# Conditions of a decoder trunk: 128x1024 blocks on GpSimd, layer 3's beside the retention, wider value products

## The chip, the cores and the metric

One core of one Trainium2 chip runs the whole kernel. The metric is device time in microseconds, the median of the runs shown. A profiled execution of the same program gives the trace.

## What is computed

A trunk of four layers over 512 tokens of width 1024, batch 1, in fp32. Layer i mixes tokens by latent attention (MLA, layers 0 and 3), stick-breaking attention (layer 1) or retention (layer 2); behind each mixer stands a dense MLP with squared ReLU and 4096 hidden units (FFN). Every mixer and FFN is wrapped in RMS norms and in a condition of the sequence: shift, scale and gate, six vectors of 1024 a layer.

```python
cond = jax.nn.silu(c)                          # (1, 1024)
for i in range(DEPTH):                         # 4
    mod = cond @ ada_w[i] + ada_b[i]           # 1024 x 6144
    sh_a, sc_a, g_a, sh_f, sc_f, g_f = jnp.split(mod, 6, axis=-1)
    h = modulate(rms_norm(x, norm_g[i, 0]), sh_a, sc_a)
    y = ...mixer(h)...
    x = x + g_a[:, None, :] * rms_norm(y, norm_g[i, 1])
    h = modulate(rms_norm(x, norm_g[i, 2]), sh_f, sc_f)
    y = jnp.square(jax.nn.relu(h @ ffn_w1[i])) @ ffn_w2[i]
    x = x + g_f[:, None, :] * rms_norm(y, norm_g[i, 3])
```

## The kernel before

**Products.** Each fp32 operand is split into a high and a low part, and each product is three TensorE matmuls into one PSUM bank (mm3, L90 to L92). A weight block of 128x1024 (512 KB) is loaded by `load_w` (L100) into a buffer `raw`, cast by ScalarE to its high part `wh` (L84), and VectorE subtracts to get the low part `wl` (L85). There are four buffers `raw`, seven each of `wh` and `wl`. Each block feeds 24 matmuls of 512 columns.

**Order.** The program is written as Python generators, and a scheduler in the build puts the instructions of each engine in an order, which the engine keeps. All DMAs of loads stand on one queue, SP's, in that order: a load that waits for its buffer holds back every load behind it. The scheduler also decides which of the four buffers a load takes.

**Conditions.** The generator `ada` runs beside a mixer or an FFN and is moved on one step (`next(bg)`) after each weight load. A group is one vector's half, 512 columns: four loads of 512 KB into `raw` (L258, two row blocks of 128x512 each), and on VectorE a multiply (L272) and seven multiply-adds (L274) into `adaacc`. `column` then transposes (L306) and reduces (L308) on VectorE, folds with a small matmul (L311) and adds the bias (L315). A gate is turned into a row by TensorE (L324), written to DRAM (L328) and read back over all partitions (L332). 44 groups run in this way; the shift and scale of the first mixer are made at the start, by the same generator in another mode. In FFN l the conditions of layer l+1 are computed. An instruction that is `held` is kept, in the scheduler's order, behind a certain matmul early in the FFN.

**Norms.** At the end of each mixer and FFN the output blocks of 128 tokens (tb 0 to 3) pass through a norm of y and then a norm of the new x: ScalarE sums the squares (ssy, ssx, L135), GpSimd makes var and rstd (L127, L130), and VectorE scales. TensorE then transposes the normed x (xn, L365) for the next product, two blocks of tokens at a time.

**Values.** In the attention heads, `to_T` transposes the probabilities by TensorE, splits them, and `av` multiplies with the values (L876), in two halves of the queries.

Of the kernel before, what the change touches and what calls it, by code (L numbers as in the profile page):

```python
# [14 lines left out]
P = 128  # L15
# [27 lines left out]
class Trunk:  # L43
    def __init__(self, ctx, tc, ins, out, mixers):
# [13 lines left out]
        self.adap = pool("ada", 2)  # L58
# [175 lines left out]
    def ada(self, wanted):  # L234

        nc = self.nc
        groups = list(wanted)  # L240
        if not groups:
            return
        raws, due = {}, []

        def load(n):
            if n >= 4 * len(groups):
                return
            l, part, name, half = groups[n // 4]
            col = (3 * part + self.ROWS[name]) * D + half * 512
            w = self.d_ada_w[l].rearrange("(kb p) n -> p kb n", p=P)  # L250
            c = n % 4
            if self.starting:
                raws[n] = [self.u(name="adaw") for _ in range(2)]
                for i in (0, 1):
                    nc.sync.dma_start(out=raws[n][i], in_=w[:, 2 * c + i, col:col + 512])
                return
            raw = self.raw().rearrange("p (a b) -> p a b", a=2)
            nc.sync.dma_start(out=raw, in_=w[:, 2 * c:2 * c + 2, col:col + 512])  # L258
            raws[n] = [raw[:, i] for i in (0, 1)]

        load(0)
        for n in range(4 * len(groups)):
            load(n + 1)
            rv, c = raws.pop(n), n % 4
            l, part, name, half = groups[n // 4]
            if c == 0:
                a = self.adap.tile([P, 512], F32, tag="acc", name="adaacc")
# [8 lines left out]
            if due and (not self.starting or c == ST2):  # L276
                next(due[0], None)
            if c == 3:
                due[:] = [self.column(*groups[n // 4], a)]
            yield  # L280
        for _ in due[0]:
            pass
        yield

    def column(self, l, part, name, half, a):


        nc = self.nc
        if name == "G":
            dst = self.st(4, "gate")  # L290
            if half == 0:
                self.gates[l, part] = self.dp.tile([1, D], F32, tag=f"gate{l}{part}", name=f"gate{l}{part}")
        else:
            if half == 0:
                self.mods[l, part, name] = self.modp.tile([P, KB], F32, name=f"mod{l}{part}{name}")
            dst = self.mods[l, part, name][:, half * 4:half * 4 + 4]
        b = (6 * l + 3 * part + self.ROWS[name]) * KB + half * 4
        if self.starting:
            ps = self.trp()[:, 0:4]
            for j in range(4):  # L300
                nc.tensor.matmul(ps[:, j:j + 1], a[:, j * P:j * P + P], self.onesf[:, 0:1], start=True, stop=True)
            nc.vector.tensor_add(dst, ps, self.bcols[:, b:b + 4])
        else:

            aT = self.adap.tile([P, 512], F32, tag="aT", name="aT", bufs=1)
            self.held(nc.vector.transpose(aT, a))  # L306
            r = self.adap.tile([P, 16], F32, tag="ar", name="ar", bufs=1)
            self.held(nc.vector.reduce_sum(r, aT.rearrange("p (c i) -> p c i", i=32), axis=mybir.AxisListType.X))  # L308
            yield
            ps = self.trp()[:, 0:16]  # L310
            nc.tensor.matmul(ps, self.fold, r, start=True, stop=True)  # L311
# [1024 lines left out]
```

## Time and profile before

| | |
|---|---|
| median of 3 runs | 2563.69 us (2559.38 to 2564.23) |
| profiled execution | 2561.43 us, span 2559.6, mean granted clock 0.987 |
| TensorE matmul (PE) | 2443.5 us, 95%, 12003 instructions |
| VectorE (DVE) | 1601.5 us, 63% |
| ScalarE (ACT) | 1089.0 us, 43% |
| GpSimd (POOL) | 151.8 us, 6%, 319 instructions |
| read from HBM | 319.51 MB |

A busy time is the sum of an engine's instructions. The share is an average over parts of the program with different limits; what a part is limited by is read from what its engines wait for. A granted clock of 1.00 is 2.4 GHz, 0.50 is 1.2 GHz. A row of a window reads: start:end, length, then busy us and (instructions) of PE, PEld (TensorE's weight loads), DVE, ACT and POOL, then granted clock, share of the DMA engines, GB/s. A row of a timeline: start, us, engine, line, operation, out<-in, and in brackets the idle time before it with what ended it.

### The profile page before, as it was taken

To read this page: it belongs to the slowest core of one execution; us is meant where nothing else is said; L and a number is where in the kernel's file an instruction comes from. 1 tells how busy PE (TensorE), PEld (TensorE's weight loads), DVE (VectorE), ACT (ScalarE), POOL (GpSimd) and SP (SyncE) were. 2 spreads that over 40 slices of the span, in tenths; PEclk is the share of its full clock that TensorE was granted. 3 is DMA by queue.
4 is the path that set the end of the run, shared out by engine and by line. 5 is a ranking of instruction groups with operands and counts; after the bars stand their busy time and mean duration, and the time that the engine had idled before them with its cause. 6 is when DMAs were issued, how large, how long until landed. Compare 5 with 4: busy or idle time off the path is not lost. (4 is left out here: it accounts for less than half of the span.)

```text
span 2559.6 us, 31769 instructions
## 1 busy us (share of the span) xinstructions
PE 2443.5 (95%) x12003; PEld 2052.5 (80%) x12003; DVE 1601.5 (63%) x2664; ACT 1089.0 (43%) x2014; POOL 151.8 (6%) x319
## 2 busy tenths in 40 slices
PE   5989999999999999999999999999999999999998
PEld 4778787888887877878788887888778778888887
DVE  7996767656988677754644444487664576634434
ACT  6655332235665533223533334443223566633322
POOL 5101000001000100000100000100000220100000
PEclk9999999999999999999999999999999999999999
DMA  7353755534112375552322222376552312333331
GB/s 242 112 182 122 256 184 187 188 123 125 59 34 72 120 250 173 188 156 91 131 74 95 95 79 82 99 238 189 174 178 85 102 34 79 128 97 101 95 95 42
DMA packets 227066, 330.00 MB, mean 129 GB/s; under 512 B 15969, under 2 KB 115169, under 8 KB 226913
## 3 DMA queue, kind: packets, MB, share of 16 engines
q1 hardware_dynamic: 226912, 327.97, 40.4%
q8 instruction: 94, 1.54, 0.3%
q14 instruction: 60, 0.48, 0.1%
HBM read 319.51 MB, written 8.42 MB: 128 GB/s over the span
## 5 line engine op out<-in xcount | busy, mean ns | idle before, releaser
L84 ACT CAST wh<-raw 128x1024 fp32r<-128x1024 f32 (+1 forms) x356 | 372.5, 1052 | 632.1 <-PE acc L92 385.3
L85 DVE TENSOR_TENSOR wl<-raw,wh 128x1024 fp32r<-128x1024 f32 (+1 forms) x356 | 434.0, 1221 | 281.6 <-ACT wh L84 278.2
L91 PE MATMUL mmp<-hl,wh 128*128 128x512 f32 (+1 forms) x1408 | 520.8, 371 | 2.4 <-DVE hl L85 2.4
L90 PE MATMUL mmp<-hh,wh 128*128 128x512 f32 (+1 forms) x1408 | 519.7, 372 | 2.1 <-ACT snT L597 1.6
L92 PE MATMUL mmp<-hh,wl 128*128 128x512 f32 (+1 forms) x1408 | 519.6, 370 | 0.0
L90 PE MATMUL acc<-wh,h1h 128*128 128x512 f32 x1024 | 407.1, 398 | 22.1 <-DVE y L533 15.1
L92 PE MATMUL acc<-wh,h1l 128*128 128x512 f32 x1024 | 403.3, 394 | 0.0
L91 PE MATMUL acc<-wl,h1h 128*128 128x512 f32 x1024 | 402.8, 393 | 0.0
L274 DVE SCALAR_TENSOR_TENSOR adaacc<-raw,cond,adaacc 128x512 f32<-128x512 f32 x308 | 230.5, 748 | 120.1 <-DMA raw<-in_ada_w_dram 115.8
L91 PEld LDWEIGHTS mmp<-hl,wh 128*128 128x128 f32 x1408 | 265.4, 188 | 47.6 <-DVE hl L85 3.9
L90 PEld LDWEIGHTS mmp<-hh,wh 128*128 128x128 f32 x1408 | 263.6, 188 | 47.6 <-ACT snT L597 2.0
L92 PEld LDWEIGHTS mmp<-hh,wl 128*128 128x128 f32 x1408 | 265.3, 188 | 45.2
L90 PEld LDWEIGHTS acc<-wh,h1h 128*128 128x128 f32 x1024 | 195.3, 191 | 66.0 <-DVE y L533 17.4
L92 PEld LDWEIGHTS acc<-wh,h1l 128*128 128x128 f32 x1024 | 194.7, 190 | 41.4
L91 PEld LDWEIGHTS acc<-wl,h1h 128*128 128x128 f32 x1024 | 195.3, 191 | 39.3
L84 ACT CAST h1h<-relu 128x512 fp32r<-128x512 f32 (+1 forms) x144 | 82.5, 575 | 240.1 <-DVE relu L483 240.1
L90 PE MATMUL acc<-wh,oh 128*128 128x512 f32 x320 | 128.0, 402 | 5.6 <-ACT wh L84 3.1
L85 DVE TENSOR_TENSOR h1l<-relu,h1h 128x512 fp32r<-128x512 f32 (+1 forms) x144 | 90.5, 631 | 62.9 <-ACT h1h L84 62.6
L92 PE MATMUL acc<-wh,hl 128*128 128x512 f32 (+1 forms) x320 | 123.3, 389 | 5.2 <-DVE hl L85 4.3
L91 PE MATMUL acc<-wl,oh 128*128 128x512 f32 x320 | 127.1, 397 | 0.0
L127 POOL TENSOR_SCALAR var<-ssy 128x1 f32<-128x1 f32 x32 | 18.9, 590 | 1819.0 <-ACT junk L135 1819.0
L92 PE MATMUL acc<-wh,ol 128*128 128x512 f32 x320 | 126.2, 395 | 0.0
(291 smaller groups left out, 3596.6 us busy)
## 6 DMA issues: line engine op xcount, KB each, us to landing
raw<-in_ffn_w_dram SPq DMA_DIRECT2D x256, 512.0 KB
raw<-in_ada_w_dram SPq DMA_DIRECT2D x176, 512.0 KB
raw<-in_ret_w_in_dram SPq DMA_DIRECT2D x48, 512.0 KB
raw<-in_sb_w_in_dram SPq DMA_DIRECT2D x24, 512.0 KB
x<-x SPq DMA_DIRECT2D x48, 256.0 KB
adaw<-in_ada_w_dram SPq DMA_DIRECT2D x32, 256.0 KB
raw<-in_mla_w_out_dram SPq DMA_DIRECT2D x16, 512.0 KB
raw<-in_ret_w_out_dram SPq DMA_DIRECT2D x16, 512.0 KB
```

Of the source, the lines that this page charges most:

```text
L84: ins = self.nc.scalar.copy(hi, src)
L85: (engine or self.nc.vector).tensor_sub(lo, src, hi.bitcast(F32))
L90: first = self.mm = mm(ps, l[0], r[0], start=start, stop=False)
L91: mm(ps, l[0], r[1], start=False, stop=False)
L92: mm(ps, l[1], r[0], start=False, stop=stop)
L127: self.nc.gpsimd.tensor_scalar(v, ss, ss2, EPS, ALU.add, ALU.add)
L274: ins = nc.vector.scalar_tensor_tensor(a, rv[i], wcol, a, ALU.mult, ALU.add)
```

## The change

A job is now a layer's part with one to three vectors, and a block is 128 rows of one vector's whole 1024 columns: 22 vectors x 8 blocks = 176 loads of 512 KB, as many and as large as before. GpSimd multiplies a block in place by its rows' conditions and adds it to `adaacc` (1024 wide); neither is `held`. Transposes and reduces stay on VectorE, 44 each. One fold matmul serves a whole job (9 in place of 44), a gate is turned in one piece (8 in place of 16). The conditions of layer 3 (48 blocks) are computed beside the retention mixer of layer 2, 12 blocks a head, in place of its FFN. The scaling of the softmax's max goes from GpSimd to VectorE. `to_T` transposes key block by key block, and `av` is 12 matmuls of 512, 384, 256 and 128 columns (three each) in place of 18 of 256 and 128.

```diff
-        self.adap = pool("ada", 2)
+        self.adap = pool("ada", 1)
...
-            for i in range(2):
-                kb = 2 * c + i
-                wcol = self.cond[:, kb:kb + 1]
-                if kb == 0:
-                    ins = nc.vector.tensor_scalar(a, rv[i], wcol, None, ALU.mult)
-                else:
-                    ins = nc.vector.scalar_tensor_tensor(a, rv[i], wcol, a, ALU.mult, ALU.add)
-                self.held(ins)
...
+    def ada(self, jobs):
+        nc = self.nc
+        blocks = [(job, i, kb) for job in jobs for i in range(len(job[2])) for kb in range(KB)]
+        raws, due, sums = {}, [], {}
+
+        def load(n):
+            if n < len(blocks):
+                (l, part, names), i, kb = blocks[n]
+                col = (3 * part + self.ROWS[names[i]]) * D
+                raws[n] = self.raw()
+                nc.sync.dma_start(out=raws[n], in_=self.d_ada_w[l][kb * P:kb * P + P, col:col + D])
+
+        load(0)
+        for n, (job, i, kb) in enumerate(blocks):
+            load(n + 1)
+            if due and next(due[0], self) is self:
+                due.pop(0)
+            rv = raws.pop(n)
+            wcol = self.cond[:, kb:kb + 1]
+            if kb == 0:
+                a = self.adap.tile([P, D], F32, tag="acc", name="adaacc", bufs=2)
+                nc.gpsimd.tensor_scalar(a, rv, wcol, None, ALU.mult)
+            else:
+                nc.gpsimd.tensor_scalar(rv, rv, wcol, None, ALU.mult)
+                nc.gpsimd.tensor_add(a, a, rv)
+            if kb == KB - 1:
+                due.append(self.columns_of(job, i, a, sums))
+            yield
...
-        nc.gpsimd.tensor_scalar(m, m, -MLA_SCALE, None, ALU.mult)
+        nc.vector.tensor_scalar(m, m, -MLA_SCALE, None, ALU.mult)
...
+        for kbs in ((0,), (1, 3), (2,)):
+            ps = self.trp()
+            off, spans = 0, []
+            for kb in kbs:
+                start = off
+                for qb in range(kb, TB):
+                    nc.tensor.transpose(ps[:, off:off + P], rows[qb][:, kb * P:kb * P + P], self.ident)
+                    off += P
+                spans.append((kb, start, off))
+            hi, lo = self.u(F32R, "pTh"), self.u(F32R, "pTl")
+            self.split(hi[:, 0:off], lo[:, 0:off], ps[:, 0:off])
...
+        for kb, r in enumerate(pT):
+            self.mm3(ps[:, kb * P:512], V[kb], r, kb == 0, kb == TB - 1)
...
+            background()
             k = rotated(hd, D)
+            background()
...
             og = mix(sc, V, sg)
-            for _ in range(6):
-                next(bg, None)
...
+        beside = {0: [(0, 0, ("G",)), (0, 1, ("sh", "S"))]}
+        for l in range(1, len(mixers)):
+            if mixers[l - 1] == "ret":
+                beside[l - 1] = beside.get(l - 1, []) + [(l, p, ("sh", "S", "G")) for p in (0, 1)]
```

The scheduler's order moves with it, at two places that matter here. The first is SP's queue in the FFN of layer 0, in the third of its four quarters: loads of conditions (in_ada_w) and of weights (in_ffn_w2, in_ffn_w1), with the engines whose work each waits for. Before, condition loads wait for a buffer that VectorE frees:

```order
L258 DMA raw_3927<-in_ada_w_dram 128x2x512 [waits DMAHW3_49,DVE_49]
L100 DMA raw_3961<-in_ffn_w2_dram 128x2x512 [waits DMAHW0_49,DVE_49]
L258 DMA raw_3967<-in_ada_w_dram 128x2x512 [waits DMAHW5_49,DVE_49]
L100 DMA raw_3995<-in_ffn_w2_dram 128x2x512 [waits DMAHW2_49,DVE_49]
L258 DMA raw_4001<-in_ada_w_dram 128x2x512 [waits DMAHW7_49,DVE_49]
L100 DMA raw_4033<-in_ffn_w1_dram 128x4x256 [waits DMAHW4_49,DVE_49]
```

After, in the second quarter of the same FFN:

```order
L300 DMA raw_3337<-in_ada_w_dram 128x1024 [waits DMAHW3_49,Pool_49]
L100 DMA raw_3347<-in_ffn_w1_dram 128x4x256 [waits DMAHW6_49,DVE_49]
L300 DMA raw_3353<-in_ada_w_dram 128x1024 [waits DMAHW5_49,Pool_49]
L100 DMA raw_3421<-in_ffn_w1_dram 128x4x256 [waits DMAHW0_49,DVE_49]
L300 DMA raw_3427<-in_ada_w_dram 128x1024 [waits DMAHW7_49,DMAHW5_49,Pool_49]
L100 DMA raw_3432<-in_ffn_w1_dram 128x4x256 [waits DMAHW2_49,DVE_49]
```

What moved: a condition's load waits for GpSimd (Pool) to be done with the block before it, in the same buffer. Before, 34 steps in a row in the FFN of layer 0 have this form, condition after condition in one buffer; after, 27 steps in three runs (10, 10 and 7), and 19 in the FFN of layer 1; in the other steps conditions and weights change buffers.

The second place is GpSimd's queue at the end of layer 1's FFN, where the norms of the last two token blocks (ssy of y, ssx of x) lead to the retention. Before:

```order
L127 TENSOR_SCALAR var_11439<-ssx_11434 128x1
L130 TENSOR_TENSOR rstd_11440<-var_11439,mhalf_125 128x1
L127 TENSOR_SCALAR var_11463<-ssy_11035 128x1
L130 TENSOR_TENSOR rstd_11464<-var_11463,mhalf_125 128x1
L127 TENSOR_SCALAR var_11474<-ssx_11469 128x1
L130 TENSOR_TENSOR rstd_11475<-var_11474,mhalf_125 128x1
```

After:

```order
L313 TENSOR_SCALAR raw_11345<-raw_11345,cond_103 128x1024
L314 TENSOR_TENSOR adaacc_11339<-adaacc_11339,raw_11345 128x1024
L127 TENSOR_SCALAR var_11032<-ssx_11027 128x1
L130 TENSOR_TENSOR rstd_11033<-var_11032,mhalf_125 128x1
L127 TENSOR_SCALAR var_11056<-ssy_10628 128x1
L130 TENSOR_TENSOR rstd_11057<-var_11056,mhalf_125 128x1
L313 TENSOR_SCALAR raw_11429<-raw_11429,cond_103 128x1024
L314 TENSOR_TENSOR adaacc_11339<-adaacc_11339,raw_11429 128x1024
L313 TENSOR_SCALAR raw_11433<-raw_11433,cond_103 128x1024
L127 TENSOR_SCALAR var_11067<-ssx_11062 128x1
L130 TENSOR_TENSOR rstd_11068<-var_11067,mhalf_125 128x1
L314 TENSOR_TENSOR adaacc_11339<-adaacc_11339,raw_11433 128x1024
```

What moved: blocks of layer 3's conditions stand ahead of and between the var and rstd of the norms. At the ends of the first MLA and of the stick-breaking mixer it is the same with the first blocks for the FFN behind them.

## Rows read from the trace of the kernel before

**Rows 1.** The page: costliest groups (busy us, mean ns | idle before) and DMA issues.

```profile
L274 DVE SCALAR_TENSOR_TENSOR adaacc<-raw,cond,adaacc 128x512 f32<-128x512 f32 x308 | 230.5, 748 | 120.1 <-DMA raw<-in_ada_w_dram 115.8
...
raw<-in_ffn_w_dram SPq DMA_DIRECT2D x256, 512.0 KB
```

**Rows 2.** What TensorE waited for: us, times, longest.

```profile
PE acc L90 <- DVE y L533: 15.1, 5, 5.2
...
PE trp L324 <- DVE gate L321: 10.6, 3, 4.8
...
PE acc L90 <- ACT wh L84: 3.1, 1, 3.1
```

**Rows 3.** Windows: FFN 0, 1, retention heads, FFN 2, 3, first and last MLA's heads.

```profile
221.60:593.00 371.40, 362.75 (x1697) 302.04 (x1696) 254.49 (x402) 128.05 (x204) 7.68 (x14) 0.99 0.55 174
861.10:1234.50 373.40, 360.70 (x1690) 301.08 (x1689) 246.84 (x387) 130.72 (x208) 7.74 (x14) 0.99 0.51 162
1290.00:1600.00 310.00, 306.42 (x1432) 256.24 (x1432) 142.86 (x194) 111.45 (x180) 13.22 (x32) 0.99 0.27 85
1648.30:2025.90 377.60, 362.62 (x1698) 302.39 (x1697) 242.65 (x397) 131.16 (x210) 7.75 (x14) 0.99 0.50 158
2199.40:2551.10 351.70, 351.09 (x1646) 294.71 (x1645) 149.04 (x189) 121.26 (x185) 5.80 (x10) 1.00 0.29 89
76.80:158.10 81.30, 74.47 (x429) 63.55 (x430) 80.16 (x192) 56.56 (x140) 9.17 (x23) 0.98 0.42 129
2068.50:2138.20 69.70, 68.39 (x420) 60.90 (x421) 51.13 (x124) 54.22 (x134) 1.56 (x7) 1.00 0.01 3
```

**Rows 4.** TensorE's timeline in FFN 0, at the wait for y.

```profile
389.18 0.79 PE L90 MATMUL acc<-wh,h1h 128*128 128x512 f32 x1 [5.20 <-DVE y L533]
```

**Rows 5.** Window behind that wait.

```profile
388.10:394.90 6.80, 5.72 (x14) 4.47 (x15) 5.16 (x8) 0.00 (x0) 0.00 (x0) 0.50 0.66 207
```

**Rows 6.** TensorE's groups by shape: the folds.

```profile
L311 PE MATMUL trp<-ar,fold 128*128 128x16 f32 x88 | 13.1, 225 | 2.9 <-DVE relu L483 1.2 <-DVE pTl L85 1.1 <-DVE ar L308 0.6
```

**Rows 7.** TensorE's timeline, one head's value products in the last MLA.

```profile
2105.99 0.42 PE L876 MATMUL mmp<-pTh,vh 128*128 128x256 f32 x2
...
2108.17 0.40 PE L90 MATMUL mmp<-lath,wh 128*128 128x512 f32 x1
```

**Rows 8.** GpSimd's timeline at the start (start, us, operation).

```profile
7.67 0.52 POOL L1258 MEMSET mask<- 128x512 f32 x1
8.26 0.29 POOL L1258 TENSOR_SCALAR_AFFINE_SELECT mask<-mask 128x128 f32<-128x128 f32 x1
...
34.96 8.75 POOL L1258 TENSOR_TENSOR hl<-ht,hh 128x256 fp32r<-128x256 f32 x8
...
56.06 0.19 POOL L129 TENSOR_SCALAR var<-ssq 128x1 f32<-128x1 f32 x1 [1.68 <-ACT junk L135]
...
67.27 0.69 POOL L791 TENSOR_SCALAR wh<-wh 128x64 fp32r<-128x64 f32 x2
```

**Rows 9.** VectorE's timeline beside those eight adds.

```profile
33.06 6.90 DVE L1258 SCALAR_TENSOR_TENSOR adaacc<-adaw,cond,adaacc 128x512 f32<-128x512 f32 x7
```

**Rows 10.** SP's timeline, condition loads at MLA 0's end, in FFN 0 and FFN 2.

```profile
195.17 0.37 SPq L258 DMA_DIRECT2D raw<-in_ada_w_dram  x1
...
301.54 0.37 SPq L258 DMA_DIRECT2D raw<-in_ada_w_dram  x1
...
381.76 0.37 SPq L258 DMA_DIRECT2D raw<-in_ada_w_dram  x1
...
1756.73 0.37 SPq L258 DMA_DIRECT2D raw<-in_ada_w_dram  x1
```

**Rows 11.** VectorE's timeline, the multiply-adds that wait for the last of them.

```profile
1760.77 1.54 DVE L274 SCALAR_TENSOR_TENSOR adaacc<-raw,cond,adaacc 128x512 f32<-128x512 f32 x2 [0.49 <-DMA raw<-in_ada_w_dram]
```

**Rows 12.** GpSimd's timeline, FFN 1 to retention.

```profile
1243.95 0.60 POOL L127 TENSOR_SCALAR var<-ssx 128x1 f32<-128x1 f32 x1 [2.40 <-ACT junk L135]
```

**Rows 13.** TensorE's timeline there: transposes of normed x.

```profile
1248.28 1.47 PE L365 MATMUL trp<-ident,xn 128*128 128x128 f32 x12
```

More of the change, by code (lines that the diff above doesn't have):

```diff
@@ L232, with ada_start, column @@
     ROWS = {"S": 1, "sh": 0, "G": 2}
-    def ada(self, wanted):
+    def ada_start(self, wanted):
         nc = self.nc
-        groups = list(wanted)
-        if not groups:
-            return
         raws, due = {}, []
+        w = self.d_ada_w[0].rearrange("(kb p) n -> p kb n", p=P)
         def load(n):
-            if n >= 4 * len(groups):
+            if n >= 4 * len(wanted):
                 return
[L248 to L259, printed above, removed]
+            name, half = wanted[n // 4]
+            col = self.ROWS[name] * D + half * 512
+            raws[n] = [self.u(name="adaw") for _ in range(2)]
+            for i in (0, 1):
+                nc.sync.dma_start(out=raws[n][i], in_=w[:, n % 4 * 2 + i, col:col + 512])
+        def column(name, half, a):
+            if half == 0:
+                self.mods[0, 0, name] = self.modp.tile([P, KB], F32, name=f"mod00{name}")
+            dst = self.mods[0, 0, name][:, half * 4:half * 4 + 4]
+            b = self.ROWS[name] * KB + half * 4
+            ps = self.trp()[:, 0:4]
+            for j in range(4):
+                nc.tensor.matmul(ps[:, j:j + 1], a[:, j * P:j * P + P], self.onesf[:, 0:1], start=True, stop=True)
+            nc.vector.tensor_add(dst, ps, self.bcols[:, b:b + 4])
+            if name == "S":
+                nc.vector.scalar_tensor_tensor(dst, dst, 1.0, self.gcols[:, half * 4:half * 4 + 4], ALU.add, ALU.mult)
+            yield
@@ L261, in ada @@
         load(0)
-        for n in range(4 * len(groups)):
+        for n in range(4 * len(wanted)):
             load(n + 1)
             rv, c = raws.pop(n), n % 4
-            l, part, name, half = groups[n // 4]
             if c == 0:
-                a = self.adap.tile([P, 512], F32, tag="acc", name="adaacc")
+                a = self.u(name="adaacc")
             for i in range(2):
@@ new lines, in ada, with columns_of @@
+        while due:
+            if next(due[0], self) is self:
+                due.pop(0)
+            else:
+                yield
+    def columns_of(self, job, i, a, sums):
+        nc = self.nc
+        l, part, names = job
+        n = len(names)
+        if i == 0:
+            sums[job] = self.adap.tile([P, 96], F32, tag="ar", name="ar", bufs=1)
+        r = sums[job]
+        yield
+        for half in (0, 1):
+            aT = self.u(name="aT")
+            self.held(nc.vector.transpose(aT, a[:, half * 512:half * 512 + 512]))
+            self.held(nc.vector.reduce_sum(r[:, 32 * i + 16 * half:32 * i + 16 * half + 16],
+                                           aT.rearrange("p (c i) -> p c i", i=32), axis=mybir.AxisListType.X))
+            if half == 0:
+                yield
+        if i < n - 1:
+            return
+        yield
+        yield
+        ps = self.trp()[:, 0:32 * n]
+        nc.tensor.matmul(ps, self.fold, r[:, 0:32 * n], start=True, stop=True)
+        pv = ps.rearrange("p (q s) -> p s q", s=4)
+        dst = self.modp.tile([P, n * KB], F32, name=f"mod{l}{part}{names[0]}")
+        b = (6 * l + 3 * part + self.ROWS[names[0]]) * KB
+        for s in range(4):
+            rows = slice(32 * s, 32 * s + 32)
+            nc.vector.tensor_add(dst[rows], pv[rows, s], self.bcols[rows, b:b + n * KB])
+        for k, name in enumerate(names):
+            d = dst[:, k * KB:k * KB + KB]
+            if name == "G":
+                g = (4 * l + 2 * part + 1) * KB
+                nc.vector.tensor_mul(d, d, self.gcols[:, g:g + KB])
+                gate = d
+            else:
+                self.mods[l, part, name] = d
+            if name == "S":
+                g = (4 * l + 2 * part) * KB
+                nc.vector.scalar_tensor_tensor(d, d, 1.0, self.gcols[:, g:g + KB], ALU.add, ALU.mult)
+        if "G" in names:
+            yield
@@ L1150, in ret, with background @@
         self.spill_x()
+        def background():
+            for _ in range(3):
+                next(bg, None)
         for hd in range(4):
@@ L1199, in run @@
         next(setup)
-        halves = [self.ada([(0, 0, n, half) for n in ("S", "sh")]) for half in (0, 1)]
+        halves = [self.ada_start([(n, half) for n in ("S", "sh")]) for half in (0, 1)]
         rope = self.mla_tables()
```

91 lines of the change are left out of this document (19 added, 72 removed).

## Prediction

> **What bounds the kernel now.** I first read the busy shares and the costliest groups on the page, then the waits of TensorE, then windows over equal pieces of the program, then the DMA queue and GpSimd. The 308 multiply-adds of the conditions take 230.5 us of VectorE at 748 ns each, and VectorE stood idle 115.8 us ahead of them for their loads [rows 1]. TensorE is what sets the end: its largest named waits are five for VectorE's y (15.1 us) and three for the gate that is turned into rows (10.6 us); for a weight it waited once, 3.1 us [rows 2]. So the conditions cost what VectorE is late by, and little else.
>
> How much that is, is read by comparing the four FFNs, which do the same 256/4 = 64 weight loads [rows 1]. Layer 3's has no conditions beside it: 351.7 us, TensorE busy 351.09. With conditions they take 371.4, 373.4 and 377.6 us [rows 3]. The excess is 19.7, 21.7 and 25.9 us. A part is the pace after a wait: behind the 5.2 us for y before 389.18 the granted clock is 0.50 (1.2 GHz), and 14 matmuls fill 6.8 us [rows 4, 5]. In the same way the heads of the first MLA, beside which conditions run, take 81.3 us and those of the last, without, 69.7: an excess of 11.6 [rows 3].
>
> **What goes.** Layer 3's conditions leave FFN 2: it should come near 351.7. I leave it 3 us, for the pass into another mixer, which FFN 3 has not: -23. In FFN 0 and FFN 1 the multiply-adds leave VectorE, so the waits for y and the gate go, while table work and folds stay: of 19.7 and 21.7 I take 16 each, -32. In the first MLA VectorE is relieved, but its chain through the softmax stays (and takes the max's scaling): half of 11.6, -6. Folds: 44 matmuls (88 records, 13.1 us of modelled time, 225 ns with overlap [rows 6]) become 9; those in the FFNs lie in the terms above, and for the rest I take -2. The products with the probabilities: in MLA the 18 matmuls of a head took from 2105.99 to 2108.17, 2.18 us [rows 7]; the columns stay 3 x (512+384+256+128) = 3840. At FFN 3's pace (351.7 us for 64 x 24 matmuls of 512 columns, 0.23 us each) the 3 x 1152 wide columns take 1.56 us, and three 128-wide ones 0.11 each, 1.89 in all: 0.29 x 16 heads = -4.6. But the first bank that is split is now 512 wide, where it was 384, and the product with the low part is second instead of third; at VectorE's 748 ns for 512 that is 0.1 to 0.3 us later per head. I take half back: -2.5. In the stick-breaking heads other products stand between split and use: nothing. The wider loads move the same bytes: nothing, since queue time is set by what frees the buffers.
>
> **What comes: the pace of a block.** On GpSimd a block is a multiply in place and an add, 128x1024 each, which no row shows. Bounds for the multiply: a memset of 512 took 0.52 us (1.0 us for 1024); the 64-wide scalings took 0.69 us for two, the 1-element ones 0.19, so 2.4 ns an element, 2.65 us. For the add: 256 wide 1.09 us (8.75/8), so 4.4 us [rows 8]. But those eight ran against VectorE, whose multiply-adds beside them took 6.90/7 = 0.99 us, against 748 ns [rows 1, 9]: they alternated, and the 1.09 us of a pair less some 0.65 for VectorE's turn (an estimate: its 748 ns without the overlap of neighbours) leave 0.45 us for 256, or 1.8 ns an element, 1.9 us for 1024. I take 2.4 for the add, nearer the low end, as VectorE works on two SBUF operands for only part of an FFN, and 1.4 for the multiply, by the select of 128 in 0.29 us, which reads one operand: 3.8 us a block against 1.5 on VectorE for the same bytes. With 176 blocks GpSimd is busy 670 us of 2540: enough on the average.
>
> The Trainium skill, GPSIMD Engine Reference, section 3.1, has an add of 2048 fp32 at 4497 ns on GpSimd and 2293 on VectorE: an estimate of 2.25 us for 1024; section 4.1 says to keep elementwise work on VectorE. With 2.25 the sum below would be some 4 us lower. No row here shows a wide add on an undisturbed GpSimd.
>
> **Where the pace counts.** All loads stand on SP's queue in order and share four raw buffers, so a weight waits behind a condition's load that waits for its buffer. In FFN 0 of before, successive condition loads take one buffer, and 14 steps from 301.54 to 381.76 are 5.73 us each [rows 10]: 4.04 from issue at 1756.73 to the multiply-add at 1760.77 [rows 10, 11], two multiply-adds of 1.54, and 0.15. That hardly delays TensorE, which wants a weight every 351.7/64 = 5.5 us. After, 27 steps in FFN 0 and 19 in FFN 1 have this form (ada waits for Pool, in the order's rows). A step is now 4.04 + 3.8 + 0.35 for two hand-overs = 8.2 us. The other steps alternate buffers; I give them 4.7, between the load (4.04) and TensorE's 5.5. The first ada load goes out at 195.17, 26 us ahead of the FFN's start [rows 10], a weight needs 6 us from issue to use, and the 57th weight follows the last serial step: 27 x 8.2 + 26 x 4.7 - 26 + 6 = 324 us, where TensorE wants it at 56 x 5.5 = 308: 16 us late. In FFN 1 the same sum (17 serial steps past the start, 30 others: 260 us for the 52nd weight, wanted at 281) leaves slack; 2 us for local bunching. Together +18. With bounds for a block of 2.9 and 7.05 us (step 7.3 and 11.4) this is 0, or 102 + 34.
>
> **Waits behind blocks.** The norms' var and rstd stand on GpSimd too, now between blocks. Before, the last var there starts at 1243.95, as soon as ScalarE's sum is there [rows 12]; the twelve transposes that end the turn ran from 1248.28 to 1249.75 [rows 13], some 2 us behind that norm's rstd and scaling. At this place (FFN 1 to retention) each of three blocks of 3.8 us must pass ahead of the last rstd, partly in gaps of some 2.4 us: about 8 us late, less the 2 of slack, +6. At MLA 0 to FFN 0 and stick-breaking to FFN 1, +4 each (three blocks in gaps of the same kind); in the first MLA's latent norms, +4, since TensorE waits on that chain already; +2 for the slower clock behind such waits. Together +20. What is late next there is the turn of the tokens' last block, then all FFN products of its columns.
>
> In retention 48 blocks x 3.8 = 182 us of GpSimd stand in some 310 us, during which VectorE is busy 142.86 us and TensorE 306.42 [rows 3]: covered, unless SP bunches; its first four loads share a buffer. +4, between 0 and 15.
>
> **Sum.** The profiled execution took 2561.4 us (span 2559.6), 2.3 under the median of the three runs. -23 - 32 - 6 - 2 - 2.5 + 18 + 20 + 4 = -23.5: 2538, at the level of the median **2540 us**.
>
> **Rivals.** (a) GpSimd is slower than I take it, and weights bound FFN 0. In favour: the 256-wide adds at 1.09 us, and VectorE's subtracts, with two operands in SBUF, for every weight. Against: those adds were in contention. Each us of a step costs 27 us in FFN 0, so from a step of 9.1 (a block of 4.7 us) on nothing is gained, and at 10.2 the time is 2540 + 27 x 2 + 6 = 2600: slower. (b) Everything hides: step 7.5, no late weights (-18), half the norm waits (-10), all of the MLA's excess (-5): 2507. For it speaks that TensorE's order leaves other work ahead of the turns; against, that the rstd chain has no cover left but 2 us. (c) Sharing of the port slows VectorE: beside GpSimd's adds its multiply-adds took 0.99 against 0.75 [rows 1, 9]. If 136 of FFN 3's 189 VectorE instructions (an estimate, the 64 subtracts among them) each waited out half of one on GpSimd, that is 136 x 0.95 = 129 us more on VectorE's 149 [rows 3]: 278 us, above FFN 0's 254 of before, so its lateness for y stays and the 32 of FFN 0 and 1 is not gained: 2572. The Trainium skill, SBUF — State Buffer, "The single rule", says a VectorE instruction with two SBUF inputs contends with a GpSimd one that reads SBUF; the alternation agrees with it.
>
> **Chances.** Forecast 0.48, (b) 0.22, (a) 0.20, (c) 0.10. What a measurement of this kernel can tell from no change is 0.2%, 5 us. The forecast's own range is 2517 to 2562 (step 7.4 to 9.0); it holds 0.42 faster, 0.05 same, 0.01 slower; (b) is faster; (a) 0.18 slower and 0.02 same; (c) 0.06 and 0.04. Together faster 0.64, same 0.11, slower 0.25. The range of 8 in 10 reaches from 2495 (all of (b), with 12 us more from the terms halved above) to 2600 (a step of 10.2).
>
> **What would show it.** FFN 2 near 352 us without waits for y or gate; FFN 0 with waits of TensorE for weights towards its end (near 16 us in sum) and a cadence of 8.2 us between condition loads in one buffer; GpSimd's multiply near 1.4 and add near 2.4 us; the last rstd at FFN 1 to retention some 8 us later against the end of the products; retention near 310 us. Wrong it would be above all by GpSimd's pace, then by a scheduler's order that bunches loads where I took them as spread.

## The result, and the profile after

The changed kernel takes 2928.4 us (2923.28 to 2929.0, four runs), 1.1424 times the 2563.44 us of the kernel before (95% interval 1.1409 to 1.1439). Its profiled execution has a span of 2927.2 us and a mean granted clock of 0.932, against 0.987.

The page of the changed kernel, busy shares and the groups that answer to [rows 1]:

```profile
PE 2509.0 (86%) x11733; PEld 2081.3 (71%) x11733; DVE 1476.1 (50%) x2173; ACT 1086.1 (37%) x2006; POOL 1077.9 (37%) x633
...
L313 POOL TENSOR_SCALAR raw<-raw,cond 128x1024 f32<-128x1024 f32 x154 | 483.0, 3137 | 314.7 <-DMA raw<-in_ada_w_dram 274.9
...
L314 POOL TENSOR_TENSOR adaacc<-adaacc,raw 128x1024 f32<-128x1024 f32 x154 | 390.5, 2536 | 11.6
```

GpSimd multiplies in 3.14 us and adds in 2.54, 5.67 us a block. VectorE got rid of work (1601.5 to 1476.1 us), and no engine is near its limit over the span; TensorE fell from 95% to 86%. What it waited for, as the views of waits put it:

```profile
PE mmp L90 <- DVE relu L528: 62.0, 8, 23.8
PE acc L90 <- DVE y L578: 45.1, 4, 13.3
PE acc L90 <- ACT h1h L84: 30.5, 6, 15.2
```
```profile
DVE wl L85 <- ACT wh L84: 814.1, 265, 20.1
```
```profile
SPq L100 <- DVE wl L85: 972.5, 193, 80.7
SPq L300 <- POOL adaacc L314: 626.2, 91, 11.5
SPq L100 <- POOL adaacc L314: 263.8, 51, 8.9
```

The engines that TensorE's rows name were late themselves. Here is its longest wait, with VectorE's timeline and SP's ahead of it:

```profile
702.07 0.79 PE L90 MATMUL mmp<-hh,wh 128*128 128x512 f32 x1 [23.78 <-DVE relu L528]
```
```profile
700.19 1.23 DVE L85 TENSOR_TENSOR wl<-raw,wh 128x1024 fp32r<-128x1024 f32 x1 [20.07 <-ACT wh L84]
701.33 0.68 DVE L528 TENSOR_TENSOR relu<-mmp,relu 128x512 f32<-128x512 f32 x1
```
```profile
679.06 14.93 SPq L300 DMA_DIRECT2D raw<-in_ada_w_dram  x4
```

The relu ended at 702.01; in VectorE's order it stood behind the subtract `wl` of a weight whose high part came 20 us late, since SP held four loads of conditions ahead of that weight. The other two views say the same of the whole span. VectorE stood 814 us waiting for a weight's high part (278.2 before, on the page), and SP's queue stood 626 us on loads of conditions that waited for GpSimd, and another 264 us on 51 loads of weights that waited for GpSimd themselves. One step of FFN 0 shows how; SP's, GpSimd's and ScalarE's timelines between 389 and 407 us:

```profile
389.54 0.33 SPq L300 DMA_DIRECT2D raw<-in_ada_w_dram  x1
389.96 0.39 SPq L100 DMA_DIRECT2D raw<-in_ffn_w_dram  x1
399.76 0.33 SPq L300 DMA_DIRECT2D raw<-in_ada_w_dram  x1
400.18 0.39 SPq L100 DMA_DIRECT2D raw<-in_ffn_w_dram  x1
```
```profile
393.90 2.85 POOL L313 TENSOR_SCALAR raw<-raw,cond 128x1024 f32<-128x1024 f32 x1 [4.38 <-DMA raw<-in_ada_w_dram]
396.83 2.90 POOL L314 TENSOR_TENSOR adaacc<-adaacc,raw 128x1024 f32<-128x1024 f32 x1
```
```profile
395.18 1.05 ACT L84 CAST wh<-raw 128x1024 fp32r<-128x1024 f32 x1 [7.23 <-DMA raw<-in_ffn_w_dram]
405.62 1.04 ACT L84 CAST wh<-raw 128x1024 fp32r<-128x1024 f32 x1 [6.75 <-DMA raw<-in_ffn_w_dram]
```

The block is issued at 389.54, lands 4.4 us later, is multiplied and added until 399.73, and the next one goes into the same buffer at 399.76: 10.2 us. The weight behind it comes at the same pace, one in 10.2 us, where TensorE uses one in 5.5.

Windows of the same stages as [rows 3] (the start to the end of the first MLA, FFN 0, FFN 1, the retention layer, FFN 2):

```profile
0.00:264.60 264.60, 181.36 (x880) 150.51 (x880) 172.11 (x318) 132.07 (x305) 185.31 (x159) 0.90 0.47 150
264.60:772.50 507.90, 387.12 (x1674) 317.27 (x1673) 207.56 (x246) 130.72 (x214) 297.77 (x116) 0.87 0.40 125
...
1046.30:1527.90 481.60, 385.49 (x1672) 315.73 (x1671) 211.68 (x250) 134.94 (x217) 262.70 (x106) 0.89 0.40 126
1527.90:2042.80 514.90, 427.72 (x1903) 351.00 (x1902) 248.40 (x315) 158.49 (x279) 264.87 (x135) 0.92 0.38 124
2042.80:2397.90 355.10, 354.50 (x1673) 297.74 (x1672) 158.75 (x222) 132.67 (x207) 7.47 (x14) 1.00 0.31 97
```

FFN 0 takes 507.9 us: 120.8 us TensorE does nothing, and its 387.1 busy us are 36 more than the 351.1 of FFN 3 [rows 3], the clock being granted at 0.87 between the two levels. FFN 2, without conditions, is at 355.1.

By stages, for all kernels of this study (us from the end of one stage to the end of the next in the profiled execution; a stage ends 0.23 us behind the start of the last product of its output; SB is the stick-breaking layer, RET the retention):

| | MLA 0 | FFN 0 | SB | FFN 1 | RET | FFN 2 | MLA 3 | FFN 3 | median |
|---|---|---|---|---|---|---|---|---|---|
| before | 221.6 | 372.1 | 267.5 | 374.1 | 413.1 | 378.3 | 172.8 | 352.4 | 2563.44 |
| after | 264.6 | 508.0 | 273.8 | 481.6 | 514.9 | 355.1 | 168.7 | 352.4 | 2928.4 |
| e1_vector | 216.1 | 355.6 | 268.9 | 360.9 | 427.9 | 355.1 | 168.4 | 352.4 | 2512.43 |
| e2_vector_l3_ffn | 215.1 | 356.4 | 268.2 | 364.2 | 412.2 | 358.2 | 167.1 | 352.4 | 2503.38 |
| e3_no_multiply | 238.0 | 397.7 | 270.2 | 396.7 | 462.4 | 355.1 | 166.8 | 352.4 | 2645.89 |
| e4_own_buffers | 310.1 | 455.0 | 269.0 | 425.9 | 453.3 | 355.1 | 171.4 | 352.4 | 2798.89 |
| e5_products_only | 222.1 | 371.2 | 268.7 | 372.9 | 414.3 | 377.7 | 168.6 | 352.4 | 2558.54 |
| e6_narrow_ops | 221.2 | 356.0 | 268.2 | 361.2 | 412.1 | 359.8 | 168.5 | 352.4 | 2512.95 |
| e7_single_jobs | 219.7 | 356.4 | 268.7 | 362.2 | 414.0 | 360.9 | 168.5 | 352.4 | 2512.43 |
| e8_own_acc3 | 314.7 | 457.2 | 271.7 | 422.8 | 448.6 | 355.1 | 169.3 | 352.4 | 2801.31 |
| e9_constant_multiply (one run) | 261.2 | 508.0 | 273.8 | 483.1 | 504.6 | 355.1 | 167.1 | 352.4 | 2915.28 |
| e10_scalar_mult | 234.1 | 387.4 | 269.6 | 381.7 | 460.8 | 355.1 | 167.1 | 352.4 | 2620.4 |
| e12_gpsimd_only | 300.9 | 577.7 | 272.0 | 540.1 | 428.4 | 534.5 | 169.6 | 352.4 | 3181.41 |
| e13_own_alternate | 261.7 | 396.4 | 279.1 | 404.1 | 482.4 | 355.1 | 169.0 | 352.4 | 2710.42 |
| e15_before_alternate | 230.7 | 361.1 | 270.2 | 363.3 | 413.4 | 365.0 | 170.5 | 352.4 | 2531.95 |
| e16_vector_own | 226.3 | 355.5 | 269.5 | 355.6 | 412.1 | 356.0 | 170.5 | 352.4 | 2506.32 |

The loss is made where GpSimd works on conditions: MLA 0 +43, FFN 0 +136, FFN 1 +108, RET +102. FFN 2 gives 23.

### The profile page after: what moved, and what is told of

It reads as the page before. It is cut to its first block, busy times and chain, and to the rows that moved or that the text cites. A ratio compares the mean times of both kernels' runs of the same rounds, so it can differ in the third digit from the quotient of the medians.

```text
span 2927.2 us, 30961 instructions
## 1 busy us (share of the span) xinstructions
PE 2509.0 (86%) x11733; PEld 2081.3 (71%) x11733; DVE 1476.1 (50%) x2173; ACT 1086.1 (37%) x2006; POOL 1077.9 (37%) x633
## 5 line engine op out<-in xcount | busy, mean ns | idle before, releaser
L85 DVE TENSOR_TENSOR wl<-raw,wh 128x1024 fp32r<-128x1024 f32 (+1 forms) x356 | 484.4, 1363 | 814.8 <-ACT wh L84 814.1
L84 ACT CAST wh<-raw 128x1024 fp32r<-128x1024 f32 (+1 forms) x356 | 372.9, 1052 | 1016.0 <-DMA raw<-in_ffn_w_dram 468.2
L90 PE MATMUL mmp<-hh,wh 128*128 128x512 f32 (+1 forms) x1408 | 532.5, 382 | 97.9 <-DVE relu L528 62.0
L313 POOL TENSOR_SCALAR raw<-raw,cond 128x1024 f32<-128x1024 f32 x154 | 483.0, 3137 | 314.7 <-DMA raw<-in_ada_w_dram 274.9
L91 PE MATMUL mmp<-hl,wh 128*128 128x512 f32 (+1 forms) x1408 | 532.4, 379 | 11.2 <-DVE hl L85 10.9
L92 PE MATMUL mmp<-hh,wl 128*128 128x512 f32 (+1 forms) x1408 | 529.9, 377 | 0.8 <-DVE wl L85 0.8
L314 POOL TENSOR_TENSOR adaacc<-adaacc,raw 128x1024 f32<-128x1024 f32 x154 | 390.5, 2536 | 11.6
L90 PEld LDWEIGHTS mmp<-hh,wh 128*128 128x128 f32 x1408 | 271.7, 194 | 152.1 <-DVE relu L528 65.4
L127 POOL TENSOR_SCALAR var<-ssy 128x1 f32<-128x1 f32 x32 | 16.5, 516 | 937.0 <-ACT junk L135 936.0
L91 PEld LDWEIGHTS mmp<-hl,wh 128*128 128x128 f32 x1408 | 273.8, 195 | 58.7 <-DVE hl L85 13.2
L311 POOL TENSOR_SCALAR adaacc<-raw,cond 128x1024 f32<-128x1024 f32 x22 | 64.1, 2916 | 392.6 <-DMA raw<-in_ada_w_dram 369.4
L85 DVE TENSOR_TENSOR h1l<-relu,h1h 128x512 fp32r<-128x512 f32 (+1 forms) x144 | 112.7, 786 | 82.0 <-ACT h1h L84 82.0
L90 PE MATMUL acc<-wh,hh 128*128 128x512 f32 (+1 forms) x320 | 127.4, 401 | 16.7 <-DVE sct L1143 13.4
```

The costliest lines, as they stand in the source:

```text
L84: ins = self.nc.scalar.copy(hi, src)
L85: (engine or self.nc.vector).tensor_sub(lo, src, hi.bitcast(F32))
L90: first = self.mm = mm(ps, l[0], r[0], start=start, stop=False)
L91: mm(ps, l[0], r[1], start=False, stop=False)
L92: mm(ps, l[1], r[0], start=False, stop=stop)
L127: self.nc.gpsimd.tensor_scalar(v, ss, ss2, EPS, ALU.add, ALU.add)
```

## The experiments

**GpSimd's work back on VectorE (e1), and layer 3's conditions back in FFN 2 (e2).** The first edit, on the changed kernel; e2 also leaves out the two lines that move layer 3.

```diff
-                nc.gpsimd.tensor_scalar(a, rv, wcol, None, ALU.mult)
+                self.held(nc.vector.tensor_scalar(a, rv, wcol, None, ALU.mult))
             else:
-                nc.gpsimd.tensor_scalar(rv, rv, wcol, None, ALU.mult)
-                nc.gpsimd.tensor_add(a, a, rv)
+                self.held(nc.vector.scalar_tensor_tensor(a, rv, wcol, a, ALU.mult, ALU.add))
```

Expected of e1: 

> The change with the conditions' multiply and add back on VectorE (1024 wide, held as before); wide blocks, merged folds, wide value products and layer 3's place beside the retention stay. Theory A (GpSimd's block of 5.7 us, in series with a 4 us load in the same buffer, holds up the weights behind it): a block is 1.5 us again, FFN 0 and FFN 1 return to 370 to 376 us, FFN 2 stays at 355, the retention layer at 413 to 425, the first MLA at 215 to 222; 2535 to 2550 in all. Theory B (the new order of loads, wide rows or the place beside the retention is at fault, whoever multiplies): FFN 0 and the retention stay above 430 and 450, over 2700 in all.

Expected of e2: 

> As the run before, but layer 3's conditions stay in layer 2's FFN, as in the kernel before. Both theories: FFN 2 back at 375 to 380 and the retention at 410 to 415; against the run before this costs 10 to 23 us if the retention hides VectorE's work, and nothing if it doesn't. About 2550 to 2560.

e1 took 2512.43 us, 0.9799 of before (0.9784 to 0.9813); e2 2503.38 us, 0.9765 (0.9743 to 0.9786). So all of the loss, 416 us, goes with GpSimd's part, and the rest of the change is worth 50 to 60 us, more than theory A had. The edit also brings back `held`; no run has VectorE's operations without it, so what `held` does by itself isn't shown. Two parts of what I expected failed. The FFNs came not to 370 but to 355.6 and 360.9, though VectorE does all the multiply-adds:

```profile
216.10:571.60 355.50, 354.90 (x1674) 297.32 (x1672) 235.27 (x298) 127.98 (x203) 7.74 (x14) 1.00 0.57 182
```

And the place beside the retention doesn't pay: FFN 2 loses 3.1 us when it gets the conditions back, the retention gains 15.7. e2 has the lowest time of the study.

**Without the multiply (e3).** The multiply is left out in blocks 1 to 7.

```diff
-                nc.gpsimd.tensor_scalar(rv, rv, wcol, None, ALU.mult)
                 nc.gpsimd.tensor_add(a, a, rv)
```

> The change without GpSimd's multiply in blocks 1 to 7 of a vector (the sum is then of unscaled rows; this leaves out the conditions' scaling). Theory A: a block is 2.5 us, a step in one buffer 4.0 + 2.5 + 0.3 = 6.8 us, 27 of them and 26 others of 5.0 less 20 us are 294 us, before the 308 at which TensorE wants the 57th weight: FFN 0 and FFN 1 at 353 to 365, the retention near 425, 2530 to 2570 in all. Theory C (GpSimd's hold on the port it shares with VectorE slows VectorE, and so the weights): adds remain and have two operands in SBUF, so at least half of the loss stays, over 2720.

2645.89 us, 1.0317 (1.0302 to 1.0333). The multiply accounts for 282 of the 416 us; the time lies between the two theories. Blocks of 2.6 us follow one another in one buffer at some 6.6 us (SP's timeline):

```profile
333.56 0.33 SPq L300 DMA_DIRECT2D raw<-in_ada_w_dram  x1
...
340.29 0.33 SPq L300 DMA_DIRECT2D raw<-in_ada_w_dram  x1
...
346.78 0.33 SPq L300 DMA_DIRECT2D raw<-in_ada_w_dram  x1
```

That step I had right (6.8), but the sum with it gave no late weights, and FFN 0 and FFN 1 lose 42 and 36 us against e1: the sum itself, not the multiply alone, was too kind.

**Buffers of their own (e4), a third accumulator (e8), and loads one for one (e13).** e4 gives the conditions two buffers and leaves two to the weights. e8 adds to e4 `bufs=3` for `adaacc` and takes two of 52 general buffers. e13 adds to e4 that a condition's load is placed behind the last weight's:

```diff
-        self.rawp = pool("raw", 4)
+        self.rawp = pool("raw", 2)
+        self.crawp = pool("craw", 2)
...
-        dma = self.nc.sync.dma_start(out=rv, in_=src)
+        dma = self.lastw = self.nc.sync.dma_start(out=rv, in_=src)
...
-                raws[n] = self.raw()
+                raws[n] = self.crawp.tile([P, 1024], F32, tag="craw", name="craw")
+                dma = nc.sync.dma_start(out=raws[n], in_=...)
+                if self.lastw is not None:
+                    self.after(dma, self.lastw)
```

Expected of e4: 

> The change with two raw buffers for conditions alone and two for weights, in place of four for both; GpSimd's work is the same. Theory A: the load of a block runs beside the block before it, a step is GpSimd's 5.7 to 6.0 us, 56 x 5.9 - 26 = 304 us: FFN 0 at 355 to 375, FFN 1 at 353 to 370, the retention at 420 to 445; 2590 to 2640 in all. Theory B' (GpSimd's pace alone is the bound, whatever the buffers): FFN 0 above 450, over 2800 in all. Theory C: as B', GpSimd's work and its hold on the port being the same.

Expected of e8: 

> The run with two raw buffers for conditions and two for weights, GpSimd multiplying (2799), with three accumulators in place of two and two fewer of the 52 general buffers. There a step was 5.3 us, but after each vector GpSimd waited some 18 us for VectorE's transposes of the vector before (303 us in all), which stand in VectorE's order behind work on weights that SP had not fetched yet. If that hand-over is the second wait, a third accumulator takes most of it: FFN 0 at 370 to 400, FFN 1 at 365 to 390, 2620 to 2700 in all. If GpSimd's pace alone is the bound: no change, 2780 to 2810.

Expected of e13: 

> The run with two raw buffers for conditions and two for weights (2799), with each condition's load kept behind the last weight's load in SP's order, so that they alternate one for one; there they stood two to one in stretches, and weights came every 10.6 us. GpSimd's work is the same. Theory A, with the order: a step is GpSimd's 5.3 to 5.7 us, about TensorE's 5.5: FFN 0 at 360 to 390, FFN 1 at 358 to 380, the first MLA still at 260 to 310; 2620 to 2700 in all. Theory B' (GpSimd's pace alone is the bound): 2780 to 2810, as before.

e4 took 2798.89 us (1.0906, 1.0888 to 1.0924). The step fell as theory A has it, but the time fell by 130 us only, to theory B's side: FFN 0 at 455.0 is above its 450, and MLA 0 even rises, to 310.1. SP's timeline shows why:

```profile
406.83 0.38 SPq L101 DMA_DIRECT2D raw<-in_ffn_w_dram  x1
411.69 5.64 SPq L301 DMA_DIRECT2D craw<-in_ada_w_dram  x2
417.43 0.38 SPq L101 DMA_DIRECT2D raw<-in_ffn_w_dram  x1
```

The two loads of the x2 row go out 5.3 us apart, GpSimd's pace, but the scheduler's order now has two of them to a weight, and the weights again come 10.6 us apart. GpSimd waited 303 us for VectorE to transpose the accumulator; a third one changed nothing (e8: 2801.31 us, 1.0938, 1.0921 to 1.0956; the same wait at 269 us). My reading of that wait was wrong: a third accumulator doesn't remove it, and in e13, where the weights come sooner, it is 23.5 us. So it followed from the late weights and did not cause them. With the loads one for one, e13 took 2710.42 us (1.0565, 1.0537 to 1.0592):

```profile
382.98 0.33 SPq L302 DMA_DIRECT2D craw<-in_ada_w_dram  x1
383.40 0.39 SPq L102 DMA_DIRECT2D raw<-in_ffn_w_dram  x1
388.29 0.33 SPq L302 DMA_DIRECT2D craw<-in_ada_w_dram  x1
388.71 0.39 SPq L102 DMA_DIRECT2D raw<-in_ffn_w_dram  x1
```

FFN 0 goes from 508.0 to 455.0 with own buffers and to 396.4 with the order, though GpSimd does the same work (296 us in that window, 298 in the changed kernel):

```profile
261.70:658.10 396.40, 363.97 (x1674) 303.26 (x1673) 205.78 (x247) 132.08 (x214) 296.03 (x119) 0.97 0.52 161
```

So 112 of the 152 us that FFN 0 loses against e1 are the shared buffer and the order of loads. The other 40 stay; e13 missed the upper end of theory A by 10 us, FFN 0 by 6 and FFN 1 (481.6, 425.9, 404.1) by 24. Over the whole kernel e13 takes off 218 of the 416 us. Against e1 it still loses 46 us in MLA 0, 41 in FFN 0, 10 in SB, 43 in FFN 1 and 55 in the retention.

**What the multiply costs (e9), and ScalarE for it (e10).** In e9 the constant 0.5 takes the place of the column (`nc.gpsimd.tensor_scalar(rv, rv, 0.5, None, ALU.mult)`); in e10 ScalarE multiplies (`nc.scalar.activation(rv, rv, AF.Copy, scale=wcol)`).

Expected of e9: 

> The change with the constant 0.5 in place of the condition's column in GpSimd's multiply of blocks 1 to 7 (this leaves out the conditions' scaling; instructions, buffers and order stay). If the operand that differs by partition makes the multiply cost 2.85 us undisturbed, it falls towards the pace of a 512-wide memset, to 1.0 to 1.6 us, and the time to 2700 to 2760. If reading, multiplying and writing 1024 elements cost it, whatever the factor: 2.8 to 3.1 us, and 2915 to 2940.

Expected of e10: 

> The change with the blocks' multiply on ScalarE (1.05 us, as its cast of the same size) and the add on GpSimd (2.4). A block in one buffer is 4.0 + 1.05 + 2.4 + 0.5 = 8.0 us, in 16, 7 and 13 steps in place of 27, 19 and 11; beyond that ScalarE's multiply waits in order for a block's landing with the weights' casts behind it. Theory A (series of load and block): FFN 0 and FFN 1 at 375 to 410, 2600 to 2680 in all. If the adds on GpSimd alone set the loss, as in the run without multiply: near its 2646.

e9 ran once: 2915.28 us, as the second alternative has it. The views of the multiply's line, of the changed kernel and of e9, give the shortest, the median and the longest in ns:

```profile
L313 POOL TENSOR_SCALAR raw<-raw,cond x154: 2839/2852/4412, 57.3 to 1901.4; 128x1024 f32<-128x1024 f32 x154
```
```profile
L313 POOL TENSOR_SCALAR raw<-raw x154: 2762/2776/3838, 57.3 to 1890.3; 128x1024 f32<-128x1024 f32 x154
```

The factor costs 0.08 us; the multiply of 1024 is 2.8 us by itself. e10 took 2620.4 us, 1.0218 (1.0202 to 1.0235), in theory A's range, with FFN 0 and FFN 1 at 387.4 and 381.7: with the multiply on ScalarE and only the add on GpSimd most of the loss goes, but the kernel stays slower than before. The steps in one buffer also fall in number there (16, 7 and 13), so it is not the block's price alone.

**GpSimd alone, on the kernel before (e12).** The two operations of 128x512 go to GpSimd, unheld; the groups made at the start (`self.starting`) stay as they were.

```diff
-                    ins = nc.vector.tensor_scalar(a, rv[i], wcol, None, ALU.mult)
+                    ins = (nc.vector if self.starting else nc.gpsimd).tensor_scalar(a, rv[i], wcol, None, ALU.mult)
+                elif self.starting:
+                    ins = nc.vector.scalar_tensor_tensor(a, rv[i], wcol, a, ALU.mult, ALU.add)
                 else:
-                    ins = nc.vector.scalar_tensor_tensor(a, rv[i], wcol, a, ALU.mult, ALU.add)
-                self.held(ins)
+                    nc.gpsimd.tensor_scalar(rv[i], rv[i], wcol, None, ALU.mult)
+                    ins = nc.gpsimd.tensor_add(a, a, rv[i])
+                if self.starting:
+                    self.held(ins)
```

> The kernel before with nothing changed but the engine: multiply and add of the conditions' 128x512 pieces on GpSimd, not held. GpSimd's part of the change then stands alone. 39, 34 and 32 steps in FFN 0, 1 and 2 have one buffer, of 4.0 + 2 x (1.47 + 1.25) + 0.5 = 9.9 us against 5.5: FFN 0 at 500 to 540, FFN 1 and FFN 2 at 490 to 530, the first MLA at 255 to 270; 2920 to 3010 in all. If the loss came from an interplay with wide blocks or the place beside the retention: under 2800.

3181.41 us, 1.2406 (1.2384 to 1.2428): the place was right, the size was above the range. FFN 0, 1 and 2 take 577.7, 540.1 and 534.5, and MLA 0 300.9. A piece's multiply and add took 1.69 and 1.41 us on the mean, where I had 1.47 and 1.25. The wide blocks and the place beside the retention don't make the loss.

**The rest of the change, part by part (e5, e6, e7).** e5 is the kernel before with `to_T`, `av` and the max's scaling of the change. e6 is e2 with each block's operation as two of 512 columns. e7 is e2 with every vector a job of its own (`jobs = [(l, part, (name,)) for l, part, names in jobs for name in names]`).

Expected of e5: 

> The kernel before with the wider value products, their transposes, and the max's scaling on VectorE, and nothing else of the change. The last MLA, which has no conditions beside it, came down from 172.8 to 167 to 169 us in the runs so far; with twice that, minus 8 to 11 us: 2552 to 2557. If the prediction's -2.5 was right, 2560.

Expected of e6: 

> The run with all on VectorE and layer 3 in its FFN (2503), with each 1024-wide multiply-add as two of 512: the loads, folds and gates stay. Theory W (its gain over the kernel before comes from VectorE's shorter work, 154 x 1.28 for 308 x 0.75 us): most of the FFNs' 16 to 20 us each comes back, 2535 to 2550. Theory F (it comes from fewer folds, bias adds and gate turns, for which TensorE stands in order): 2503 to 2512.

Expected of e7: 

> The same run (2503) with every vector a job of its own: 22 folds in place of 9 and 88 bias adds in place of 36; blocks stay 1024 wide, gates are turned in one piece. Theory F: a good part of the gain goes, 2515 to 2530. Theory W: 2503 to 2508.

e5: 2558.54 us, 0.9982 (0.9967 to 0.9997). e6: 2512.95 us. e7: 2512.43 us. The products are worth some 4 us (1 to 8 by the interval), less than I expected: MLA 3 gets 4.2 us shorter, MLA 0 doesn't. The wide operations and the merged folds are worth some 9 us each against e2, about half of it in MLA 0 (221.2 and 219.7 against 215.1). That is near the noise: against before the ratios are 0.981 (0.9793 to 0.9828) and 0.9803 (0.978 to 0.9827), and e2's interval reaches to 0.9786. Neither W nor F explains the 10 to 20 us that each FFN gained in e2: there e6 and e7 stay within 3 us of e2.

**What the FFNs of the kernel before waited for (e15), and the best version with it (e16).** e15 is the kernel before with two and two buffers and loads kept apart as in e13. e16 is e2 with the same.

Expected of e15: 

> The kernel before with two raw buffers for its conditions' loads and two for weights, each condition's load kept behind the last weight's; the conditions stay on VectorE, narrow, with 44 folds. If the FFNs' excess of 20 to 26 us over the last one came from the runs of condition loads in one buffer (33, 20 and 17 steps of 5.7 us against TensorE's 5.5, VectorE waiting in order for each landing), it goes here as it did in the runs with all on VectorE (356 to 364): FFN 0, 1 and 2 at 354 to 362, 2505 to 2525 in all. If it came from the 44 folds and gates: 365 to 378, 2545 to 2565.

Expected of e16: 

> The best version so far (conditions on VectorE in wide blocks, layer 3's in its FFN, 2503) with the same two and two buffers and order. By the first account of the run beside it the FFNs come to 353 to 358 from 356 to 364: 2490 to 2500. If buffers no longer matter there: 2500 to 2510.

e15: 2531.95 us, 0.9877 (0.9849 to 0.9904), with FFNs of 361.1, 363.3 and 365.0: 11 to 13 us less than before, of the 10 to 20 that e2 gained, on the same narrow operations and 44 folds; MLA 0 gives 9 us back. The waits of VectorE for conditions, in the kernel before and in e15:

```profile
DVE adaacc L274 <- DMA raw<-in_ada_w_dram: 115.8, 65, 4.2
```
```profile
DVE adaacc L278 <- DMA craw<-in_ada_w_dram: 63.3, 48, 2.5
```

e16: 2506.32 us, 0.9779 (0.9755 to 0.9803), no better than e2: its FFNs are at 355.5 to 356.0, and MLA 0 (226.3) loses what they gain.

## Why the prediction was wrong

**The first step that failed is the pace of a block, in it the price of the multiply.** I took 1.4 us for the multiply, by the select of 128 columns, which reads one operand as the multiply does. It takes 2.85 us undisturbed and 3.14 on the mean. The upper bound of 2.65, from 64-wide scalings, was the nearer row, since those are the same operation on the same engine, and even it was too low. The add was right: 2.4 foreseen, 2.34 at the least and 2.54 on the mean measured; the estimate of 2.25 from the figure in the Trainium skill (GPSIMD Engine Reference, section 3.1) is near it. With 5.67 us a block the step is 10.2, as my sum for a step gives it (4.04 + 5.67 + 0.35 = 10.1).

**The second step, and the larger, is the sum that turns this pace into late weights.** At a step of 10.2 it gave 2600 us. At the 8.2 that I forecast it gave 16 and 2 us for FFN 0 and FFN 1, which lose 152 and 121 against e1. For a block of 2.6 us, less than the 3.8 that I assumed, e3 shows 42 and 36 us lost there, where my sum has none. Two terms were wrong. The other steps, which I gave 4.7 us, cannot be shorter than GpSimd's own block of 5.67. And the 26 us of lead was no lead: after four loads of conditions SP's queue stood still, but for one weight, and the fifth went out at 295 us, 30 us into the FFN (24 in e3). With 10.2 us for 27 steps, 6.0 for the other 26 and no lead, my sum gives 129 us late in FFN 0 in place of 16, an estimate from these numbers.

The queue stands still at that place in other kernels too. SP's timelines of e1 and of e13:

```profile
213.50 0.38 SPq L100 DMA_DIRECT2D raw<-in_ffn_w_dram  x1
235.87 0.33 SPq L300 DMA_DIRECT2D raw<-in_ada_w_dram  x1
```
```profile
264.96 0.45 SPq L302 DMA_DIRECT2D craw<-in_ada_w_dram  x1
293.36 0.38 SPq L102 DMA_DIRECT2D raw<-in_ffn_w_dram  x1
```

In e1 the conditions' loads then follow every 3.6 us at first, and TensorE waits for none of it. In e13 they follow every 6.2 us at first, where TensorE wants a weight every 5.5: the delay isn't made up, and 24.3 of the 32.4 us that TensorE idles in FFN 0 lie in its first 98 us. This is read from the traces; no run takes the standstill away.

TensorE's pace was left out too. In FFN 0 it idles 120 us more than in e1, and its same 1674 matmuls are busy for 32 us more (387.1 against 354.9), at a granted clock of 0.87 against 1.00. Whether these 32 us add to the waits for weights or pass beside them isn't shown. Rival (a), with 0.20, had the mechanism and the sign; its price, 2600, holds a tenth of the loss.

**The 32 us for the FFNs: right in size, wrong in cause.** In e1 the two FFNs gain 16.5 and 13.2 us with the multiply-adds still on VectorE. I read y's lateness as VectorE's work. The timeline of the kernel before shows VectorE idle just ahead of y, in order, waiting for a block to land:

```profile
385.72 1.54 DVE L274 SCALAR_TENSOR_TENSOR adaacc<-raw,cond,adaacc 128x512 f32<-128x512 f32 x2 [2.85 <-DMA raw<-in_ada_w_dram]
387.18 1.22 DVE L85 TENSOR_TENSOR wl<-raw,wh 128x1024 fp32r<-128x1024 f32 x1
388.43 1.29 DVE L533 TENSOR_TENSOR y<-acc,y 128x512 f32<-128x512 f32 x2
```

With the loads in one buffer at 5.73 us against TensorE's 5.5, VectorE comes later step by step until y is late. e15 shows that this is the larger part. The program of e2 has 18, 10 and 13 steps in one buffer in the three FFNs, that of before 33 (the 34 loads in a row of the order above), 20 and 17; that this count is what differs is argued from e15, not shown by itself. In the changed kernel the gain is there and buried under the weights.

**Waits behind blocks: +20 foreseen, more measured.** MLA 0 was to gain 2 on balance and loses 43; e1 has 216.1, so GpSimd costs 48 there. GpSimd's timeline in the latent norms:

```profile
81.20 0.19 POOL L129 TENSOR_SCALAR var<-sskv 128x1 f32<-128x1 f32 x1
81.49 2.89 POOL L313 TENSOR_SCALAR raw<-raw,cond 128x1024 f32<-128x1024 f32 x1
84.35 0.56 POOL L130 TENSOR_TENSOR rstd<-var,mhalf 128x1 f32<-128x1 f32 x1
84.89 2.35 POOL L314 TENSOR_TENSOR adaacc<-adaacc,raw 128x1024 f32<-128x1024 f32 x1
```

A block's multiply stands even between var and its rstd, and the eight norms there, of which the first began at 56.06 in the kernel before [rows 8] and the last ended at 65.3, now begin at 68.2 and end at 96.0. I had counted the blocks and taken only 4 us, since TensorE waited there already. The turns were later as well. At stick-breaking to FFN 1, with 4 us foreseen, TensorE waits 2.92, 2.27 and 4.84 us, where in e1 none of its waits there is above 0.61. At FFN 1 to the retention the last var starts 22.2 us behind the end of the products (1550.10), before 8.7: 13.5 later, 8 foreseen.

**Retention: +4 foreseen, +102 measured.** "Covered, unless SP bunches" was the wrong bound. Near its start SP holds four loads of conditions in a row for 17.5 us ahead of the weights:

```profile
1541.87 17.49 SPq L300 DMA_DIRECT2D raw<-in_ada_w_dram  x4
1564.75 9.91 SPq L100 DMA_DIRECT2D raw<-in_ret_w_in_dram  x4
```

Of the 102 us, 15 come with the place alone (e1: 427.9), the other 87 with GpSimd. With GpSimd's same work, conditions' buffers of their own bring the stage to 453.3 (e4) and the loads one for one to 482.4 (e13), so buffers and order hold 33 to 62 of these 87. What the rest is, norms behind blocks or the pace itself, was not tried.

**Right.** FFN 2: -23 foreseen, -23.2 measured. Value products: -2.5 foreseen, some 4 us measured, which the noise doesn't tell apart (e5).

**Open or off by a little.** Folds: -2 foreseen for those outside the FFNs; single jobs cost some 9 us in all (e7), half of it in MLA 0. Rival (c): VectorE's subtracts grew from 1221 to 1363 ns on the mean, longest 3448; but in e13, where they take 1347 and GpSimd works as long, FFN 0 is 112 us shorter, so the port is not the main cause. Its part in the 40 us that stay in e13, beside the delay at the start, is open. Two readings of the prediction are off and change little. Among TensorE's largest waits it leaves out 14.8 us at the start, for the first mixer's scale, with which GpSimd's part has nothing to do. And the 0.99 us of (c) are a mean of seven: three multiply-adds took 0.75, the four between GpSimd's adds 1.09 to 1.11.

## What to carry to other kernels

An engine that shares buffers and an in-order DMA queue with the critical stream is not off the path because it has idle time: add its work to the load into the same buffer and compare the step, not the share, with the pace of the stream. Price an operation that no row shows by rows of the same operation, however small, before rows of another one. And where a wait names an engine, look at what that engine itself waited for just before; here it was a load each time, in the kernel before as in the one after. Last, a queue's lead is worth only what its later pace keeps of it.

## What was not expected of the hardware

On GpSimd the multiply of 128x1024 fp32 by a column, in place, is slower (2.85 us) than the add of two such tiles (2.34 to 2.40 undisturbed), and a constant in place of the column saves only 0.08 us. Beside VectorE's work the multiply took up to 4.41 us, and VectorE's subtract of the same size up to 3.45 us against 1.23 in the kernel before.
